# The first FFN's weights are split with ScalarE and adding GpSimd transfers instead of VectorE

## The chip, the core and the metric

The kernel runs on one core of a Trainium2 chip. The metric is device time in microseconds (us) for one execution. Engines are named as in the profile: PE is TensorE, PEld its weight loads, DVE is VectorE, ACT is ScalarE, POOL is GpSimd, SP is SyncE (which here only issues transfers).

## The reference

Two transformer stacks follow each other on 512 tokens of 1024 channels. The part that the change touches is the first of three convolutional FFNs:

```
D_MODEL = 1024; SEQ = 512; D_FF = 2816; CONV_WIDTH = 3
def conv_ffn(x_n, w_up, conv_w, w_down):
    g, u = jnp.split(causal_dwconv(x_n @ w_up, conv_w), 2, axis=-1)
    return (jax.nn.silu(g) * u) @ w_down
...
h = h + short_conv_mixer(rms_norm(h, a_mix_norm[layer]), ...)
h = h + conv_ffn(rms_norm(h, ffn_norm[layer]), ffn_w_up[layer], ffn_conv[layer], ffn_w_down[layer])
```

Behind it come a latent attention, the second FFN, a second block with three mixers, the third FFN and a last norm. All of it is fp32.

## The kernel before

Every matrix product is made of three products with rounded operands. A weight w is split into hi (w rounded to fp32r) and lo = w - hi, an activation x likewise, and PE adds hi·xh, lo·xh and hi·xl into one PSUM bank (`mm3`, L149 to L151; xh and xl are `xsh` and `xsl`, or `hidh` and `hidl`). Tokens lie along the 512 columns of a matmul, channels on the 128 partitions.

Weights come through `slab` (L127 to L145). One SP transfer brings a slab of up to 2048 columns into `raw` (two buffers). Each piece of it is cast by ACT into `whi` (L139) and subtracted by DVE into `wlo` (L141). The pool `wsp` holds two buffers of each, so a piece can be split only when PE is through with the piece two before it.

`ffn(0)` takes its work in two halves of the hidden channels. In the first half it takes 12 slabs of `w_up0` (24 pieces of 1024 columns, each the 8 chunks of one 128-row tile of the product, 24 matmuls) and 8 slabs of `w_down0` (one piece of 1408 columns each, 33 matmuls). In the second half it takes 10 slabs of `w_up0` (20 pieces) and 8 of `w_down0`. That is 60 pieces in all. In this text they are called piece 1 to piece 60 in the order of the code. The last slab of `w_down0` goes to a pool of its own, `late0`. An `evac` behind each tile of `w_up0` multiplies by the norm's factor (DVE), convolves (ACT and DVE), applies silu and splits the hidden rows. In the first half, and at the start of the second, `work` also brings rows of `w_ada` (`ada`, 512 KB each, on SP's queue) and reduces them on DVE (L461).

The order of each engine's instructions is set by the Tile scheduler, which places instructions by priority and by its own estimate of times. Each engine then takes its own list strictly in order. An instruction that waits holds up all that stands behind it on its engine, and for SP and GpSimd these are the transfers that they issue.

Of the kernel before, what the change touches and what calls it, by code (L numbers as in the profile page):

```python
# [19 lines left out]
# What is put between the heads of the stick-breaking attention: slabs of w_out_ac (negative: into a bank  # L20
# of the logits) and weights of what follows.
# [26 lines left out]
class Builder:  # L48
    def __init__(self, ctx, tc, dr, out):
        self.tc, self.nc, self.dr, self.out = tc, tc.nc, dr, out  # L50
        nc = self.nc
        self.ctx = ctx
        self.const = self.pool("const", 1)
        self.wraw = self.pool("wraw", 2)
        self.wsp = self.pool("wsp", 2)
        self.tmp = self.pool("tmp", 1)
        self.small = self.pool("small", 2)

        nc.scalar.preload_act_table(AF.Silu)
        self.par = self.const.tile([P, NPAR], F32, name="par")  # L60
        self.ident = self.const.tile([P, P], F32, name="ident")
        nc.sync.dma_start(self.par[:, :32], dr["params"][:, :32])
        self.mod = self.const.tile([P, 48], F32, name="mod")
        self.probs, self.zms, self.dns = [None] * 6, [None] * 3, [None] * 3
        self.rbs = [None] * 2
        self.hold, self.bufs = None, {}
        self.ones = self.const.tile([P, 1], F32, name="ones")
        nc.vector.memset(self.ones, 1.0)
        self.mhalf = self.const.tile([P, 16], F32, name="mhalf")
        nc.vector.memset(self.mhalf, -0.5)  # L70
        self.h = [self.const.tile([P, T], F32, name=f"h{c}") for c in range(KC)]
# [31 lines left out]
    # Exact two-part split: hi holds 12 significant bits, lo the rest.  # L103
# [23 lines left out]
    def slab(self, src, piece, pool=None, width=PIECE):  # L127
        nc = self.nc
        n = src.shape[-1]
        raw = self.wraw.tile([P, SLAB], F32, tag="raw", name="raw")  # L130
        nc.sync.dma_start(raw[:, :n], src)
        for o in range(0, n, piece):
            own = pool[o // piece] if type(pool) is tuple else pool or self.wsp
            hi = own.tile([P, width], F32R, tag="whi", name="whi")
            lo = own.tile([P, width], F32R, tag="wlo", name="wlo")
            m = min(piece, n - o)
            s = slice(o, o + m)
            with self.tc.issue_after(self.rounded) if self.hold else nullcontext():
                nc.scalar.copy(hi[:, :m], raw[:, s])  # L139
# [13 lines left out]
    def add3(self, ps, wh, wl, xh, xl, first=False):  # L153
        """Onto what products left in the bank, unless it is the first."""
# [4 lines left out]
    def gemm(self, w, xs, evac, slabs=None, group=1, m=0, tag="ps", pool=None):  # L159
        """w: [slabs, 128, m-tiles of a slab x chunks x 128]; evac(m, psum) takes each m-tile from m on."""  # L160
# [11 lines left out]
    def gemm_first(self, w, xs, evac, n):  # L172
        """n m-tiles side by side, their chunks taken as xs yields them."""
# [9 lines left out]
    # Around a norm the tokens go in two halves: one's factors are worked out under the other's products.  # L183
# [3 lines left out]
    def chunks(self, slabs):  # L187
        """The weights of 128 columns after 128 columns, split."""
        return [(hi[:, o:o + P], lo[:, o:o + P]) for hi, lo, n in slabs for o in range(0, n, P)]

    def gemm_halves(self, w, xs, evac):
        """The first m-tiles, chunk by chunk; w: weights by m-tile and chunk, xs[half] yields that half
        of the chunks."""
# [13 lines left out]
    def gemm_last(self, w, xs, evac, done):  # L207
        """The last m-tiles, half by half; w[m]: the weights of each chunk."""
# [10 lines left out]
    def act(self, *args, **kw):  # L219
        """Exp or Ln from the table set that has both."""  # L220
# [3 lines left out]
    # Per-token factors: tokens on the partitions, [128, 4].  # L224
# [40 lines left out]
    def conv(self, x, w, i, n, bias=None):  # L265
        """Causal 3-tap convolution along the tokens; taps of channel tile i in w, n tiles a tap."""
# [20 lines left out]
    def summed(self, add, scales=(None,)):  # L287
        """add, and the squares of h (times each of scales) summed over the chunks as they come;
        those of the last chunk stay apart."""
# [23 lines left out]
    def half_sums(self, half, i=0):  # L313
        """Sums over the channels of a half: tokens on the partitions, [128, 2]."""
# [18 lines left out]
    def half_factor(self, half):  # L333
        """The factors of a half's norm, along the tokens."""
# [4 lines left out]
    def half_factors(self, half):  # L339
        """Two norms in a row: with m1 and m2 the mean squares before and after the first one's gain,  # L340
        (m2 / (m1 + eps) + eps) (m1 + eps) is m2 + eps m1 + eps^2. The first's factor is kept."""
# [52 lines left out]
    def ffn(self, i, xs, rb, add, work=None, done=None, first=None, late=None):  # L394
        """Without rb the normalised rows come whole, and the convolution has a bias."""
# [28 lines left out]
        for half, ys in enumerate(hids):  # L424
            if half:
# [24 lines left out]
    def modulation(self, steps):  # L450
        """shift, scale and gate from c: channels on the partitions, 128 of them in a step."""
# [22 lines left out]
    # Latent attention.  # L474
    def latent(self, w, small, g, dim, ctx, extra=None, pool=None):
        """Normalised latent, its chunks split. With m the mean square of the input's row and l the one
        of the row before the input's factor, (l / (m + eps) + eps) (m + eps) is l + eps (m + eps):
        small is eps (m + eps)."""
# [27 lines left out]
    def swap(self, x):  # L506
        """The halves of each 64 channels, exchanged."""
# [6 lines left out]
    def rope(self, x, cos, sin, after=None):  # L514
        """after: what the vector engine has to do before it takes up the exchanged halves."""
# [126 lines left out]
    def norm_shift(self, gain, shift):  # L642
        """The modulated norm of h, a half after the other: a generator for each."""
# [18 lines left out]
    def gemm_tok(self, w, xs, n, kp, tok):  # L662
        """Tokens on the partitions: w's slabs hold chunks x n columns, kp chunks are split at a time."""
# [12 lines left out]
    def before(self, start):  # L676
        """What is traced inside goes before what was traced since start, where both are ready."""
        return self.tc.high_priority(offset=self.tc.tile_snap_priority() - start)

    def angles(self, pool):  # L680
        """cos and signed sin of position x frequency, the angle reduced to [-pi, pi]."""
# [25 lines left out]
    def gating_in(self, xs, pool):  # L707
# [5 lines left out]
        # Two chunks at a time; the second half behind the first, within what is kept of the weights.  # L713
# [53 lines left out]
    def values(self, ps, npair, pool, tag):  # L767
        """[V of a head | 0 | V of the next] for each pair: a window of 128 columns has one of them."""
# [20 lines left out]
    # Group 0 in the order of the tokens; groups 1 and 2 by the token's rest of a division by 4,  # L789
    # which splits each into four problems of 128 by 128.  # L790
# [57 lines left out]
    def dilated_values(self, vn, vp, y_pool):  # L848
        nc = self.nc
        pool, probs, zms, dns = self.ph, self.probs, self.zms, self.dns  # L850
        # Log-sum-exps, group 0's brought to the order of the others.
# [7 lines left out]
        def reorder(x, sel, keep):  # L859
            """x [128, (head, j)] -> [128, (head, i)]: sel[i] picks rows for each j, keep the j."""  # L860
# [78 lines left out]
    def stick(self, q, k, rows, v, pair, h, out):  # L939
        """Keys on the partitions. The sums over later keys are products with triangles of -1,  # L940
        accumulated onto the logits where they lie."""
# [3 lines left out]
        for t in (2, 1, 0):  # L945
# [3 lines left out]
            # The first product clears the bank for both regions.  # L949
# [34 lines left out]
    def mixer(self, stat):  # L984
        """stat: what holds the sums behind the first norm, open until the bank can go."""
# [105 lines left out]
    def last_phase(self, y_b, wq, held, first, wf0, ctx):  # L1091
        """held: what the mixer's products need, until the last of them."""
# [29 lines left out]
    def final_norm(self, half):  # L1122
        """The rows go out as they are laid: tokens on the partitions, times their factors."""
# [22 lines left out]
    def ffn_phase(self, i, ctx):  # L1146
        self.stat = self.pool(f"stat{i}", 1, ctx, space=PSUM)
        with ExitStack() as ctx:
# [9 lines left out]
            if i == 0:  # L1158
                self.ffn(i, xs, rb, (self.add_h, self.add_h), work, late=self.pool("late0", 1, ctx))
            else:  # L1160
# [4 lines left out]
                self.modulation_end()  # L1165

# [9 lines left out]
def pack(w, per, rows=None):  # L1176
    """[K, N] -> [slabs, 128, per x K/128 x 128]: 128x128 tiles, the contraction on the partitions."""
# [104 lines left out]
```

## Time and profile before

| | before |
|---|---|
| time, median of 3 runs | 1822.06 us (1821.37 to 1825.72) |
| profiled execution, span | 1822.4 us |
| PE busy | 1796.4 us |
| DVE busy | 1110.4 us |
| ACT busy | 698.3 us |
| GpSimd busy | 19.1 us |
| HBM read | 180.27 MB |

The profiled execution is known by its span alone, from its first to its last instruction. It lies 0.3 us above the median of the runs, and no time around the span is given for it. The first FFN begins on PE at 190.1 us and its last product is over before 560 us.

### The profile page before, as it was taken

What the parts mean: (1) busy time and instruction counts of PE and PEld (TensorE: products, weight loads), DVE (VectorE), ACT (ScalarE), POOL (GpSimd) and SP (SyncE); (2) the same over time, 40 slices, a digit from 0 to 9 for tenths busy, and PEclk for the clock granted to TensorE, in tenths of its full rate; (3) what the DMA queues carried; (4) which work ended last, traced back from release to release, by engine and by line L of the source; (5) the groups of instructions that cost most, each with busy time, mean ns of one, the idle gap of its engine ahead of it and who ended that gap; (6) DMA issues with size and microseconds to landing.
All of it is one profiled execution on the core that took longest, in us unless ns stands there. A gap on an engine that the chain in (4) does not pass through costs nothing.

```text
span 1822.4 us, 20686 instructions
## 1 busy us (share of the span) xinstructions
PE 1796.4 (99%) x8301; PEld 1457.3 (80%) x8301; DVE 1110.4 (61%) x1717; ACT 698.3 (38%) x1054; POOL 19.1 (1%) x27
## 2 busy tenths in 40 slices
PE   8999999999999999999999999999999999999998
PEld 6888888888887777787788888887767988888887
DVE  4655699446754676789944775755444765525554
ACT  4323334224434454444422444423354444313432
POOL 0000000000000000000000000100000000000000
PEclk9999999999999999999999999999989999999999
DMA  6222463322231211247332224312101222222222
GB/s 221 93 92 93 162 243 120 111 92 93 94 117 62 76 58 64 99 139 242 125 99 105 93 80 140 100 60 91 61 30 45 82 76 101 81 95 92 94 97 76
DMA packets 38928, 186.59 MB, mean 102 GB/s; under 512 B 5168, under 2 KB 6192, under 8 KB 26672
## 3 DMA queue, kind: packets, MB, share of 16 engines
q1 hardware_dynamic: 36720, 182.38, 29.2%
q10 hardware_dynamic: 2112, 2.89, 0.6%
q8 instruction: 65, 1.06, 0.3%
q14 instruction: 31, 0.25, 0.0%
HBM read 180.27 MB, written 2.10 MB: 100 GB/s over the span
## 4 chain that ended last, share of the span: by engine, by line
PE 93%; DVE 3%; DMA 3%; ACT 1%; issue 1%; SPq 0%; DVEq 0%; POOLq 0%; ACTq 0%
PE ps L149 28%; PE ps L150 28%; PE ps L151 28%; DMA ada<-w_ada 2%; PE z L156 1%; PE z L973 1%; PE sc L149 1%; DVE ada L461 1%; PE o L981 1%; PE sc L151 1%; PE sc L150 1%; DVE wlo L141 1%; PE sc L837 1%; PE pt L630 1%; PE st L932 0%
## 5 line engine op out<-in xcount | busy, mean ns | idle before, releaser
L149 PE MATMUL ps<-xsh,whi 128*128 128x512 f32 (+1 forms) x1432 | 555.7, 393 | 7.9 <-ACT whi L139 6.3
L150 PE MATMUL ps<-xsh,wlo 128*128 128x512 f32 (+1 forms) x1432 | 561.5, 392 | 0.7 <-DVE wlo L141 0.7
L151 PE MATMUL ps<-xsl,whi 128*128 128x512 f32 (+1 forms) x1432 | 559.0, 392 | 0.0
L139 ACT CAST whi<-raw 128x1024 fp32r<-128x1024 f32 (+5 forms) x282 | 296.7, 1057 | 519.5 <-PE ps L151 424.0
L141 DVE TENSOR_TENSOR wlo<-raw,whi 128x1024 fp32r<-128x1024 f32 (+5 forms) x282 | 346.6, 1232 | 110.8 <-ACT whi L139 109.8
L149 PEld LDWEIGHTS ps<-xsh,whi 128*128 128x128 f32 x1432 | 270.5, 189 | 70.1 <-ACT whi L139 6.3
L150 PEld LDWEIGHTS ps<-xsh,wlo 128*128 128x128 f32 x1432 | 270.7, 189 | 64.7 <-DVE wlo L141 2.7
L151 PEld LDWEIGHTS ps<-xsl,whi 128*128 128x128 f32 x1432 | 269.7, 189 | 61.7
L150 PE MATMUL ps<-hidh,wlo 128*128 128x512 f32 (+1 forms) x658 | 244.4, 372 | 0.0
L151 PE MATMUL ps<-hidl,whi 128*128 128x512 f32 (+1 forms) x658 | 244.3, 372 | 0.0
L149 PE MATMUL ps<-hidh,whi 128*128 128x512 f32 (+1 forms) x658 | 244.2, 372 | 0.0
L149 PEld LDWEIGHTS ps<-hidh,whi 128*128 128x128 f32 x658 | 123.8, 188 | 24.0
L150 PEld LDWEIGHTS ps<-hidh,wlo 128*128 128x128 f32 x658 | 123.7, 188 | 23.8
L151 PEld LDWEIGHTS ps<-hidl,whi 128*128 128x128 f32 x658 | 123.7, 188 | 23.7
L274 DVE SCALAR_TENSOR_TENSOR cv<-e,par,cv 128x511 f32<-128x511 f32 (+1 forms) x192 | 141.3, 745 | 2.0 <-ACT cv L270 0.3
L279 DVE TENSOR_TENSOR h<-ps,h 128x512 f32<-128x512 f32 (+1 forms) x75 | 49.9, 668 | 135.3 <-PE ps L151 134.9
L274 DVE SCALAR_TENSOR_TENSOR cv<-ps,par,cv 128x511 f32<-128x511 f32 (+1 forms) x88 | 65.4, 748 | 86.8 <-ACT cv L272 85.2
L406 DVE TENSOR_TENSOR e<-ps,rb 128x512 f32<-128x512 f32 x88 | 60.0, 687 | 65.0 <-PE ps L151 65.0
L118 ACT CAST hidh<-cv 128x512 fp32r<-128x512 f32 x66 | 40.8, 618 | 125.3 <-DVE cv L414 125.3
L270 ACT ACTIVATE cv<-e,par 128x512 f32<-128x512 f32 x96 | 68.7, 719 | 25.0 <-DVE e L406 23.7
L412 ACT ACTIVATE si<-cv 128x512 f32<-128x512 f32 x66 | 41.7, 631 | 73.5 <-DVE cv L274 73.3
L283 DVE SCALAR_TENSOR_TENSOR h<-ps,mod,h 128x512 f32<-128x512 f32 (+1 forms) x38 | 23.9, 635 | 67.9 <-PE ps L151 67.9
(307 smaller groups left out, 1824.6 us busy)
## 6 DMA issues: line engine op xcount, KB each, us to landing
raw<-w_up SPq DMA_DIRECT2D x65, 1024.0 KB, 4.8
raw<-w_down SPq DMA_DIRECT2D x48, 704.0 KB, 4.1
ada<-w_ada SPq DMA_DIRECT2D x48, 512.0 KB, 4.4
raw<-a_w_in SPq DMA_DIRECT2D x9, 1024.0 KB, 4.8
raw<-a_w_out SPq DMA_DIRECT2D x4, 1024.0 KB, 4.7
raw<-w_o SPq DMA_DIRECT2D x4, 1024.0 KB, 5.2
raw<-a_w_in_first SPq DMA_DIRECT2D x8, 384.0 KB, 4.3
raw<-w_uq SPq DMA_DIRECT2D x4, 768.0 KB, 4.8
```

Of the source, the lines that this page charges most:

```text
L118: nc.scalar.copy(vh, src)
L139: nc.scalar.copy(hi[:, :m], raw[:, s])
L141: nc.vector.tensor_tensor(lo[:, :m], raw[:, s], hi[:, :m].bitcast(F32), ALU.subtract)
L149: mm(ps, wh, xh, start=first, stop=False)
L150: mm(ps, wl, xh, start=False, stop=False)
L151: mm(ps, wh, xl, start=False, stop=last)
L270: nc.scalar.activation(y, x, AF.Identity, scale=self.p(w, 2 * n + i))
L274: nc.vector.scalar_tensor_tensor(y[:, k:], x[:, :T - k], self.p(w, (2 - k) * n + i), y[:, k:], ALU.mult, ALU.add)
L279: self.nc.vector.tensor_tensor(self.h[m][:, s], ps, self.h[m][:, s], ALU.add)
L283: self.nc.vector.scalar_tensor_tensor(self.h[m][:, s], ps, self.mod[:, gate + m:gate + m + 1], self.h[m][:, s], ALU.mult, ALU.add)
L406: nc.vector.tensor_tensor(e, ps, rb, ALU.mult)
L412: nc.scalar.activation(st["s"], y, AF.Silu)
```

## The change

In `ffn(0)` alone, `slab` goes by another path. A flag `by_dma` is "rest" in the first half and "all" in the second.

- In "rest", `raw` and the ACT cast into `whi` stay. The remainder is made by ACT, which writes -hi into `wlo`, and by a transfer on GpSimd's queue, which reads the weights from HBM once more and adds them onto `wlo`.
- In "all", there is no `raw` either: a transfer on GpSimd's queue brings the weights into `whi` and rounds them on the way. The remainder is made as in "rest".
- Every third piece goes to a third pair of buffers, the new pool `wsp2`. The pool `late0` is gone. So a piece can now be split when PE is through with the piece three before it.

Other differences between the two files are comments.

```diff
-        raw = self.wraw.tile([P, SLAB], F32, tag="raw", name="raw")
-        nc.sync.dma_start(raw[:, :n], src)
+        if self.by_dma != "all":
+            raw = self.wraw.tile([P, SLAB], F32, tag="raw", name="raw")
+            nc.sync.dma_start(raw[:, :n], src)
         for o in range(0, n, piece):
             own = pool[o // piece] if type(pool) is tuple else pool or self.wsp
+            if self.by_dma and own is self.wsp:
+                self.turn += 1
+                own = self.wsp2 if self.turn % 3 == 0 else own
             hi = own.tile([P, width], F32R, tag="whi", name="whi")
             lo = own.tile([P, width], F32R, tag="wlo", name="wlo")
             m = min(piece, n - o)
             s = slice(o, o + m)
+            if self.by_dma:
+
+                if self.by_dma == "all":
+                    nc.gpsimd.dma_start(hi[:, :m], src[:, s])
+                else:
+                    nc.scalar.copy(hi[:, :m], raw[:, s])
+                nc.scalar.activation(lo[:, :m], hi[:, :m].bitcast(F32), AF.Copy, scale=-1.0)
+                nc.gpsimd.dma_start(lo[:, :m], src[:, s], accum_op=ALU.add)
...
+                continue
...
         for half, ys in enumerate(hids):
+            if i == 0:
+                self.by_dma = ("rest", "all")[half]
...
             if i == 0:
-                self.ffn(i, xs, rb, (self.add_h, self.add_h), work, late=self.pool("late0", 1, ctx))
+                self.wsp2 = self.pool("wsp2", 1, ctx)
+            if i == 0:
+                self.ffn(i, xs, rb, (self.add_h, self.add_h), work)
...
+            self.by_dma = None
```

What this makes of the engines' lists is shown at three places. In the changed file the matmuls of `mm3` are L166 to L168, the negation is L148, the adding transfer L149 and the rounding transfer L145.

**ScalarE, start of the first FFN.** `whi_1367` is piece 1 in both. Piece 2 is `whi_1404` before and `whi_1405` now; piece 3 is `whi_1452` before and `whi_1454` now. `xsh` and `sq` belong to the last chunks of the norm. Before:

```order
L139 CAST whi_1367<-raw_1365 128x1024
L120 ACTIVATE xsh_1315<-h6_85,par_71 128x512
L231 ACTIVATE sq_1340<-h6_85 128x512
L139 CAST whi_1404<-raw_1365 128x1024
L120 ACTIVATE xsh_1319<-h7_86,par_71 128x512
L231 ACTIVATE sq_1343<-h7_86 128x512
L139 CAST whi_1452<-raw_1450 128x1024
```

Now:

```order
L147 CAST whi_1367<-raw_1365 128x1024
L120 ACTIVATE xsh_1315<-h6_85,par_71 128x512
L248 ACTIVATE sq_1340<-h6_85 128x512
L148 ACTIVATE wlo_1368<-whi_1367 128x1024
L147 CAST whi_1454<-raw_1452 128x1024
L148 ACTIVATE wlo_1455<-whi_1454 128x1024
L147 CAST whi_1405<-raw_1365 128x1024
L120 ACTIVATE xsh_1319<-h7_86,par_71 128x512
L248 ACTIVATE sq_1343<-h7_86 128x512
L148 ACTIVATE wlo_1406<-whi_1405 128x1024
```

The negation of piece 1 stands behind two steps of the norm, and piece 3, whose buffers are new, is split ahead of piece 2.

**PE, a border between two pieces in the second half.** Before (`ps_2893` ends and `ps_2938` begins):

```order
L149 MATMUL ps_2893<-xsh_1319,whi_2889 128x512
L150 MATMUL ps_2893<-xsh_1319,wlo_2890 128x512
L151 MATMUL ps_2893<-xsl_1320,whi_2889 128x512
L149 MATMUL ps_2938<-xsh_1291,whi_2934 128x512
L150 MATMUL ps_2938<-xsh_1291,wlo_2935 128x512
L151 MATMUL ps_2938<-xsl_1292,whi_2934 128x512
```

Now, at the same place (`ps_2925` ends; pieces 39 and 40 are `whi_2964` and `whi_3002`):

```order
L166 MATMUL ps_2925<-xsh_1319,whi_2920 128x512
L167 MATMUL ps_2925<-xsh_1319,wlo_2921 128x512
L168 MATMUL ps_2925<-xsl_1320,whi_2920 128x512
L166 MATMUL ps_2969<-xsh_1291,whi_2964 128x512
L166 MATMUL ps_3007<-xsh_1291,whi_3002 128x512
L167 MATMUL ps_2969<-xsh_1291,wlo_2965 128x512
L168 MATMUL ps_2969<-xsl_1292,whi_2964 128x512
```

The first matmul of the second piece of a pair has moved ahead of the first use of the first piece's remainder.

**GpSimd, the same stretch.** Before, it held only norm factors and a few memsets in the whole program, and none of its instructions lay inside the second half:

```order
L244 ISA
L244 TENSOR_TENSOR r<-ms,mhalf 128x4 x6
L244 TENSOR_TENSOR r<-ms_8629,mhalf 128x2
L351 TENSOR_TENSOR r_6097<-m_8628,mhalf 128x2
L771 MEMSET vp 128x2x64 x4
```

Now (pieces 37 to 40, `whi` and `wlo` of a piece bearing neighbouring numbers):

```order
L145 DMA whi_2882<-w_up0 128x1024
L145 DMA whi_2920<-w_up0 128x1024
L149 DMA wlo_2883<-w_up0 128x1024
L149 DMA wlo_2921<-w_up0 128x1024
L145 DMA whi_2964<-w_up0 128x1024
L145 DMA whi_3002<-w_up0 128x1024
L149 DMA wlo_2965<-w_up0 128x1024
L149 DMA wlo_3003<-w_up0 128x1024
```

The adding transfer of the first piece of a pair (`wlo_2965`) stands behind the rounding transfer of the second (`whi_3002`). Pieces 37 to 52 go in eight such pairs, pieces 33 to 36 one by one.

## Rows read from the trace of the kernel before

**Rows 1.** The page's first part: busy us, share of the span, instructions

```profile
PE 1796.4 (99%) x8301; PEld 1457.3 (80%) x8301; DVE 1110.4 (61%) x1717; ACT 698.3 (38%) x1054; POOL 19.1 (1%) x27
```

**Rows 2.** Windows: stretch, length, busy of PE, PEld, DVE, ACT, POOL; clock, DMA share, GB/s

```profile
190.00:312.00 122.00, 122.00 (x533) 98.61 (x532) 105.47 (x154) 48.19 (x63) 1.01 (x1) 1.00 0.55 187
...
324.00:386.00 62.00, 62.00 (x268) 49.94 (x267) 22.74 (x23) 12.46 (x11) 0.00 (x0) 1.00 0.31 104
386.00:498.00 112.00, 112.00 (x482) 90.24 (x481) 75.59 (x95) 44.41 (x57) 0.00 (x0) 1.00 0.25 88
```

**Rows 3.** PE's waits in the whole program: total us, times, longest

```profile
PE ps L149 <- ACT whi L139: 7.2, 2, 6.3
PE st L932 <- DVE yl L123: 3.6, 1, 3.6
PE ps L149 <- ACT lath L118: 2.0, 1, 2.0
PE ps L149 <- DVE h L279: 1.8, 3, 0.9
```

**Rows 4.** Groups by shape, 184 to 560 us, DVE and ACT

```profile
L141 DVE TENSOR_TENSOR wlo<-raw,whi 128x1024 fp32r<-128x1024 f32 x46 | 56.1, 1220 | 16.0 <-ACT whi L139 16.0
...
L141 DVE TENSOR_TENSOR wlo<-raw,whi 128x1408 fp32r<-128x1408 f32 x16 | 25.9, 1625 | 8.9 <-ACT whi L139 8.7
...
L139 ACT CAST whi<-raw 128x1024 fp32r<-128x1024 f32 x46 | 48.3, 1051 | 105.6 <-PE ps L151 93.0 <-issue 12.6
...
L139 ACT CAST whi<-raw 128x1408 fp32r<-128x1408 f32 x16 | 21.9, 1374 | 59.3 <-PE ps L151 48.7 <-issue 5.2 <-DMA raw<-w_down 4.7
```

**Rows 5.** Timeline of GpSimd, and one issue on SP: start, length

```profile
200.72 1.01 POOL L244 TENSOR_TENSOR r<-ms,mhalf 128x4 f32<-128x4 f32 x1 [172.57 <-DVE ms L252]
...
608.32 1.39 POOL L244 TENSOR_TENSOR r<-ms,mhalf 128x4 f32<-128x4 f32 x1 [11.08 <-DVE ms L498]
...
218.60 0.33 SPq L131 DMA_DIRECT2D raw<-w_up  x1
```

**Rows 6.** Transfers issued 190 to 560 us: count, KB each, median us to landing

```profile
raw<-w_up SPq DMA_DIRECT2D x20, 1024.0 KB, 4.8
ada<-w_ada SPq DMA_DIRECT2D x22, 512.0 KB, 4.4
raw<-w_down SPq DMA_DIRECT2D x16, 704.0 KB, 4.1
...
raw<-w_dkv SPq DMA_DIRECT2D x1, 512.0 KB, 3.2
```

**Rows 7.** Timeline of ACT at the start of the first FFN

```profile
184.73 1.05 ACT L139 CAST whi<-raw 128x1024 fp32r<-128x1024 f32 x1 [3.39 <-issue]
185.68 0.72 ACT L120 ACTIVATE xsh<-h,par 128x512 fp32r<-128x512 f32 x1
186.31 0.62 ACT L231 ACTIVATE sq<-h 128x512 f32<-128x512 f32 x1
190.34 1.05 ACT L139 CAST whi<-raw 128x1024 fp32r<-128x1024 f32 x1 [3.42 <-PE ps L151]
```

**Rows 8.** Timeline of PE at the same border

```profile
189.85 0.39 PE L151 MATMUL ps<-hidl,whi 128*128 128x512 f32 x1
190.09 0.39 PE L149 MATMUL ps<-xsh,whi 128*128 128x512 f32 x1
```

**Rows 9.** Windows around two gaps of PE, columns as in rows 2

```profile
600.00:620.00 20.00, 17.97 (x89) 14.64 (x88) 15.13 (x25) 9.45 (x16) 1.39 (x1) 0.98 0.29 88
620.00:632.00 12.00, 11.57 (x55) 9.05 (x54) 7.76 (x14) 4.56 (x10) 0.00 (x0) 0.89 0.03 7
1320.00:1330.00 10.00, 6.37 (x46) 5.74 (x45) 5.47 (x7) 4.57 (x6) 0.00 (x0) 0.96 0.38 121
1330.00:1340.00 10.00, 10.00 (x42) 7.81 (x41) 3.64 (x7) 4.43 (x10) 0.00 (x0) 0.67 0.04 12
1340.00:1350.00 10.00, 10.00 (x40) 7.86 (x41) 5.93 (x12) 5.82 (x12) 0.00 (x0) 0.69 0.00 1
```

More of the change, by code (lines that the diff above doesn't have):

```diff
@@ L65, in __init__ @@
         self.rbs = [None] * 2
-        self.hold, self.bufs = None, {}
+        self.hold, self.bufs, self.by_dma, self.turn = None, {}, None, 0
         self.ones = self.const.tile([P, 1], F32, name="ones")
@@ L137, in slab @@
             s = slice(o, o + m)
+            if self.by_dma:
[5 more added lines that the diff above has]
+                nc.gpsimd.dma_start(lo[:, :m], src[:, s], accum_op=ALU.add)
+                if pool is None:
+                    yield hi, lo
+                else:
+                    yield hi, lo, m
+                continue
             with self.tc.issue_after(self.rounded) if self.hold else nullcontext():
```

## The prediction

> **What bounds the kernel now.** I read the page's busy times first. PE is busy 1796.4 of the 1822.4 us [rows 1], so nothing but 26 us of PE's gaps can be won by relieving another engine. A busy PE need not be at its peak, so I then cut the first FFN into windows and counted matmuls. From 190 to 312 us, where DVE is loaded most (105.5 of 122 us), from 324 to 386, where it is loaded least (22.7 of 62), and from 386 to 498, PE is busy all the time, and 112 us hold 482 matmuls: 0.232 us each, at full clock [rows 2]. The rate does not care what DVE does. Last come PE's waits in the whole program: the long ones are on the first weights of the program (7.2 us), in the second block's attention (3.6) and behind the first FFN, in the latent attention (2.0) [rows 3]. None lies in the stretch whose weights the change splits in another way. There PE uses up a piece of 24 matmuls in 5.57 us and one of 33 in 7.66, and the split keeps ahead of it.
>
> **What is removed.** DVE loses 44 subtractions of 1.220 us (the row counts 46, two belong to the next stage) and 16 of 1.625: 79.7 us [rows 4]. PE waits for none of them, so this is worth nothing by itself.
>
> **What is added off the path.** ACT gains 60 negations, costed like the casts of the same size, 44 × 1.051 + 16 × 1.374 = 68.2 us, and loses the 28 casts of the second half, 20 × 1.051 + 8 × 1.374 = 32.0 [rows 4]. In 112 us of steady state ACT is busy 44.4 [rows 2]; 20 pieces there would bring 21 more. The cover is ACT's idle time, and it holds. SP loses 18 slab loads. GpSimd, nearly empty, gets 88 transfers, and HBM is read once more for each remainder, 34 MB.
>
> **What is added on the path.** The remainder used to be ready 2.3 us after its buffer came free (a cast and a subtraction). Now it goes through a queue and a transfer. No row shows either kind of GpSimd transfer, so three prices are bounded by neighbours:
> - g, GpSimd's own time for one transfer: 0.33 us, as SP's issue, to 1.39, as its slower small power; I take 1.0, its power in this very stage, since it is the same engine [rows 5].
> - H, a 512 KB rounding transfer from there to landing: 3.2 to 4.4 us, the two plain rows of that size; I take 3.2, since the 4.4 was measured amid the `ada` traffic, which is over by then [rows 6].
> - A, a 512 KB adding transfer: 3.2 if adding is free, 9.6 at twice the 1024 KB row; I take 4.8, that row itself, because the transfer has to read 512 KB of weights and 512 KB of what it adds onto [rows 6].
>
> What the Trainium skill says of such an addition, in "Collectives: The Full Stack" (The bandwidth ceiling), is that it is not slow for the arithmetic but because it has two source reads. That fits the choice of A; no row here shows it.
>
> A handover between engines costs 0.1: a matmul that starts at 189.85 and takes 0.39 frees the buffer of a cast that starts at 190.34 [rows 7, 8].
>
> *Start of the FFN.* Piece 1's buffer comes free as before, and its cast starts at 184.73. Two norm steps follow it on ACT and end by 186.9 [rows 7]; the negation ends at 188.0, and the remainder lands at 188.0 + 0.1 + 1.0 + 4.8 + 0.1 = 194.0. PE arrives at 190.09 [rows 8], does one matmul, and then has to do one with piece 2, whose cast cannot start before 190.34 [rows 7]: ready 191.5 instead of 190.3, 1.2 lost. After two more matmuls it is 192.0, and piece 1's remainder is 2.0 late. Sum 3.2 us.
>
> *Pieces 5 to 7.* Piece 3 was taken before piece 2, so piece 5 has one piece less of lead. From the end of piece 2: cast of 5 (to 1.15), of 6 (2.2), one `evac` step of 0.72, negation (3.95), transfer: 9.95. PE meanwhile has 3 matmuls of piece 3, the 24 of piece 4, and one each of 5, 6 and 7; the one of 7 waits for a cast that needs the end of piece 4 (7.5 instead of 6.7, 0.8 lost), and then at 7.75 the remainder of 5 is 2.2 late. Sum 3.0 us.
>
> *Rest of the first half.* Three buffers give 11.1 us from a free buffer to its use. Needed are 0.1 + 1.05 + 0.72 + 1.05 + 0.1 + 1.0 + 4.8 + 0.1 = 8.9. The 2.2 to spare cover it; for 1408 columns there is more to spare. Nothing.
>
> *Second half, pairs.* GpSimd's list is in pairs: rounding a, rounding b, adding a, adding b. Rounding b waits until PE has ended the first piece of the previous pair, and adding a stands behind it. From that moment PE has 23 matmuls of the previous pair's second piece and two first matmuls: 25 × 0.232 = 5.8 us. Adding a lands after 0.1 + 2 × 1.0 + 4.8 + 0.1 = 7.0. So 1.2 us are lost in each of eight pairs: 9.6. Adding b lands in time: 0.1 + 1.0 + 3.2 + 0.1, about 0.35 of another ACT step, a negation 1.05, 0.1 + 1.0 + 4.8 + 0.1 = 11.8, wanted at 5.8 + 1.2 + 5.3 = 12.3. The same chain for pieces 33 to 36, which go one by one, takes 11.8 where 11.4 is there: three times 0.4, with what piles up at the fourth 1.5. The first pair of `w_down0` has 704 KB transfers; A grows there by the slope between the 704 and 1024 KB rows (0.7 per 320 KB, so 0.8 for the 384 KB more that it reads) to 5.6, and is 2.0 late. The later pieces have 7.4 us instead of 5.3 and lose nothing. Sum 13.1 us.
>
> Total 3.2 + 3.0 + 13.1 = 19.3 us on the profiled 1822.4: **1841.7 us**, 1.1% slower. (The median of the runs is 0.3 lower, which I leave out.)
>
> **The rivals.**
>
> *The transfers are hidden (no change).* With g 0.33 and A 3.2 the pairs need 4.1 of 5.8 us, the start 1.2, piece 5 0.8: 2.0 in all, 1824.4. It decides at 2g + A below 5.6. For it speaks that plain 512 KB loads do land in 3.2 [rows 6]; against it, that an addition has to read both operands and that GpSimd takes a microsecond for the smallest operation [rows 5]. The Trainium skill, "DMA: Bandwidth & Descriptors" (Anatomy of one DMA), would put a 512 KB GpSimd transfer at 2.0 us plus its bytes at 436 GB/s, an estimate of 3.2 us. With A at the 3.2 of the row and g at 1.0 only 3.5 us would be lost, 1825.9. Chance of this rival 0.18.
>
> *The transfers are dearer.* With g 1.39, H 4.4 and A 9.6, the start costs 8.4, piece 5 8.2, each of the 17 `w_up0` pieces from 8 to 24 one third of the 3.0 us by which its chain is too long (17), the pairs 6.8 each (54), pieces 33 to 36 about 14, the pair of `w_down0` 8: 110 us, 1932. Two things push that way. From 190 to 312 us the queues already take 0.55 of the DMA engines at 187 GB/s [rows 2], and the remainders add some 94 GB/s of reading, more where `ada` is densest; with the second reads that can fill them, and 2.2 us are all there is to spare. And a gap of PE can cost clock: after 2.5 us of gaps the granted clock was 0.89 for 12 us, and after 3.6 us it was 0.67 and 0.69 for 20 [rows 9], 1.3 and 6.4 us of work; ten gaps at 1.3 would make 13 us, 1855. Chance of 1860 or more 0.30.
>
> *Faster.* Freed of 79.7 us, DVE might bring the end of the FFN forward. Of PE's waits 1.8 us are on DVE's additions to `h`, over three places [rows 3], and in the second block the scheduler's order has changed slightly. To pass the bound of 0.3%, 5.5 us, the 3.6 us gap of the attention and the half clock behind it (6.4) would have to go as well, by an order that happens to be luckier: about 1811. Nothing in the change reaches there directly. Chance 0.06.
>
> **How the numbers follow.** 0.46 for some 1828 to 1860 around 1841.7; 0.18 hidden; 0.30 at 1860 and beyond, about a tenth of it all above 1892; 0.06 faster. About 0.3% is what a measurement of this kernel can tell from no change. Faster 0.06, same 0.18, slower 0.76. The range 1822 to 1892 leaves out about 0.1 on each side.
>
> **What would show it.** Right: in the second half of the FFN (some 370 us wide before, near 390 now) PE waits for transfers of `wlo` about once a pair, for a microsecond or two; at its start it waits for a cast and then a transfer. The landing time of the adding transfers and GpSimd's spacing of neighbouring issues give A and g. Wrong: PE without gaps there means that 2g + A is below 5.6; gaps in the steady first half mean that it is over 8 or that the `ada` traffic delays the transfers. A fall of the clock behind the gaps would be a cost that the sum has not.

## The result, and the profile after

The changed kernel takes **1900.24 us** (median of 4 runs, 1898.52 to 1912.52) against 1821.71 for the kernel before on the same chip: ratio 1.0443, 95% interval 1.0414 to 1.0471. It is 4.4% slower, 78.5 us. The prediction had the sign and most of the places, but 19.3 us, and the result lies beyond its upper bound of 1892.

The profiled execution has a span of 1896.7 us, 74.3 more than before. The busy line of the page after, and windows of the same three kinds as in [rows 2] (dense vector work, `w_down0`, second half; columns as there):

```profile
PE 1821.3 (96%) x8301; PEld 1469.5 (77%) x8301; DVE 1041.8 (55%) x1657; ACT 733.5 (39%) x1086; POOL 88.1 (5%) x115
```

```profile
190.00:312.00 122.00, 104.89 (x433) 82.76 (x434) 74.60 (x118) 56.57 (x70) 16.26 (x19) 0.94 0.94 253
345.00:405.00 60.00, 60.00 (x260) 48.53 (x259) 9.92 (x14) 20.95 (x18) 8.02 (x10) 1.00 0.84 202
425.00:545.00 120.00, 98.98 (x378) 76.26 (x376) 47.31 (x66) 38.74 (x50) 24.47 (x34) 0.91 0.65 141
```

DVE is relieved, 1110.4 to 1041.8 us [rows 1] (68.6 less, where the prediction added up 79.7), and PE does the same 8301 matmuls. But in the first and third window PE is no longer busy all the time, its granted clock is below 1, and in the first the DMA engines are busy 0.94 of the time instead of 0.55 [rows 2]. Only in the stretch of `w_down0` in the first half does PE run as before.

PE's waits in the whole program after (total us, times, longest), which answer to [rows 3]:

```profile
PE ps L167 <- DMA wlo<-w_up: 38.9, 17, 5.3
PE ps L167 <- DMA wlo<-w_down: 8.9, 4, 3.0
PE ps L166 <- ACT whi L156: 7.0, 2, 6.1
PE st L951 <- DVE yl L123: 3.6, 1, 3.6
...
PE ps L166 <- ACT whi L147: 1.6, 2, 0.9
```

The first two rows and the last are new: 49.4 us, with 0.3 more on a rounding transfer 49.7, all in the first FFN (a "gap" is from here on a wait of PE for a weight). 17.2 of it lies in the first half, 32.5 in the second. From the last addition to `h` ahead of the first FFN (at 189.70 us, before 190.28) to the first matmul behind it (632.32, before 562.30, where the last product of the FFN ends at 561.4 and not before 560) are 442.6 us instead of 372.0, 70.6 more. The gaps leave 20.9 of them. Windows of the changed kernel around one of the gaps (5.3 us, until 223.8):

```profile
215.00:219.50 4.50, 2.83 (x11) 1.72 (x10) 4.40 (x9) 3.82 (x7) 1.23 (x2) 1.00 0.98 339
219.50:229.70 10.20, 5.88 (x14) 4.68 (x15) 6.29 (x11) 1.85 (x3) 0.86 (x1) 0.50 1.03 246
229.70:240.00 10.30, 10.30 (x47) 8.41 (x46) 7.14 (x12) 4.87 (x6) 0.86 (x1) 1.00 0.87 284
```

PE waits, and the granted clock is 0.50, 1.2 GHz instead of 2.4, until well after it works again: in the middle row 14 matmuls in 5.88 us, 0.42 each, where the next row has 0.22. I cut the whole FFN into short windows and added up length × (1 - granted clock): 20.4 us, none in the kernel before. Gaps of 49.7 and 20.4 of lost clock make 70.1 of the 70.6. Behind the FFN the changed kernel takes another 4.3 us more (1264.4 against 1260.1). The same sum there is 13.6 us against 10.3, if the last stretch, in which PE has almost nothing to do, is left out; what brings the difference was not tried.

Groups by shape of the FFN after (busy us, mean ns), the prices that [rows 4] and [rows 5] stood in for:

```profile
L148 ACT ACTIVATE wlo<-whi 128x1024 fp32r<-128x1024 f32 x44 | 46.3, 1053 | 62.5 <-DMA whi<-w_up 62.3
L149 POOL DMA_DIRECT2D wlo<-w_up x44 | 38.7, 878 | 343.4 <-ACT wlo L148 342.0 <-PE ps L167 1.0 <-DMA wlo<-w_up 0.4
...
L145 POOL DMA_DIRECT2D whi<-w_up x20 | 14.0, 699 | 60.6 <-PE ps L168 51.6 <-issue 8.9
```

Transfers after, by stretch of issue (count, KB, median us from issue to landing, GpSimd's own time in it), 190 to 262 us and 425 to 545, beside [rows 6]:

```profile
ada<-w_ada SPq DMA_DIRECT2D x15, 512.0 KB, 6.2
raw<-w_up SPq DMA_DIRECT2D x6, 1024.0 KB, 6.7
wlo<-w_up POOLq DMA_DIRECT2D x11, 512.0 KB, 8.8
...
wlo<-w_up POOLq DMA_DIRECT2D x17, 512.0 KB, 5.6
whi<-w_up POOLq DMA_DIRECT2D x16, 512.0 KB, 5.7
```

In the second half, beside rounding transfers but away from the `ada` loads, an adding transfer lands after 5.6 us, amid the `ada` loads after 8.8. These loads and the raw ones have become slower themselves, 6.2 and 6.7 us, where the kernel before has in the same stretch, 190 to 262 us:

```profile
ada<-w_ada SPq DMA_DIRECT2D x17, 512.0 KB, 4.1
raw<-w_up SPq DMA_DIRECT2D x6, 1024.0 KB, 5.6
```

The timeline of the start, engine by engine, where [rows 7] and [rows 8] stood:

```profile
186.24 1.05 ACT L148 ACTIVATE wlo<-whi 128x1024 fp32r<-128x1024 f32 x1
...
187.61 1.05 POOL L149 DMA_DIRECT2D wlo<-w_up  x1 [160.06 <-ACT wlo L148]
...
190.80 0.74 PE L166 MATMUL ps<-xsh,whi 128*128 128x512 f32 x2 [0.90 <-ACT whi L147]
193.24 0.50 PE L167 MATMUL ps<-xsh,wlo 128*128 128x512 f32 x1 [1.71 <-DMA wlo<-w_up]
```

This is the forecast sequence nearly to the tenth: 0.90 on the cast of piece 2 (forecast 1.2), 1.71 on the remainder of piece 1 (2.0).

And one pair of the second half:

```profile
451.30 0.89 POOL L145 DMA_DIRECT2D whi<-w_up  x1
458.59 1.06 ACT L148 ACTIVATE wlo<-whi 128x1024 fp32r<-128x1024 f32 x1 [3.58 <-DMA whi<-w_up]
461.50 0.55 POOL L145 DMA_DIRECT2D whi<-w_up  x1 [9.31 <-PE ps L168]
462.04 0.92 POOL L149 DMA_DIRECT2D wlo<-w_up  x1
468.20 0.87 POOL L149 DMA_DIRECT2D wlo<-w_up  x1 [5.25 <-ACT wlo L148]
468.76 0.87 POOL L145 DMA_DIRECT2D whi<-w_up  x1
...
469.28 0.50 PE L167 MATMUL ps<-xsh,wlo 128*128 128x512 f32 x1 [1.90 <-DMA wlo<-w_up]
```

The negation of piece a is done at 459.65, but its adding transfer starts only at 462.04: ahead of it in GpSimd's list stands the rounding transfer of piece b, which waits until PE has left b's buffer (9.31 us of idle, ended by PE). From 461.50 to PE's first use are 7.8 us, where the prediction had 7.0. At 468.76 the next pair's rounding transfer goes out right behind adding b.

### The profile page after: what moved, and what is told of

It reads as the page before. It is cut to its first block, busy times and chain, and to the rows that moved or that the text cites. A ratio compares the mean times of both kernels' runs of the same rounds, so it can differ in the third digit from the quotient of the medians.

```text
span 1896.7 us, 20827 instructions
## 1 busy us (share of the span) xinstructions
PE 1821.3 (96%) x8301; PEld 1469.5 (77%) x8301; DVE 1041.8 (55%) x1657; ACT 733.5 (39%) x1086; POOL 88.1 (5%) x115
## 4 chain that ended last, share of the span: by engine, by line
PE 78%; issue 10%; DMA 6%; DVE 3%; POOL 2%; ACT 1%; POOLq 0%; DVEq 0%; SPq 0%; ACTq 0%
PE ps L166 23%; PE ps L167 23%; PE ps L168 23%; DMA wlo<-w_up 3%; POOL wlo L149 1%; PE z L173 1%; PE z L992 1%; POOL whi L145 1%; PE sc L166 1%; DMA ada<-w_ada 1%; DVE ada L480 1%; PE o L1000 1%; DVE wlo L158 1%; PE sc L168 1%; PE sc L167 1%
## 5 line engine op out<-in xcount | busy, mean ns | idle before, releaser
L167 PE MATMUL ps<-xsh,wlo 128*128 128x512 f32 (+1 forms) x1432 | 568.7, 397 | 39.2 <-DMA wlo<-w_up 38.9
L166 PE MATMUL ps<-xsh,whi 128*128 128x512 f32 (+1 forms) x1432 | 559.4, 396 | 10.4 <-ACT whi L156 6.1
L168 PE MATMUL ps<-xsl,whi 128*128 128x512 f32 (+1 forms) x1432 | 563.7, 395 | 0.0
L156 ACT CAST whi<-raw 128x1024 fp32r<-128x1024 f32 (+4 forms) x222 | 228.6, 1035 | 360.5 <-PE ps L168 283.8
L166 PEld LDWEIGHTS ps<-xsh,whi 128*128 128x128 f32 x1432 | 273.7, 192 | 75.4 <-ACT whi L156 6.0
L168 PEld LDWEIGHTS ps<-xsl,whi 128*128 128x128 f32 x1432 | 273.2, 191 | 61.5
L158 DVE TENSOR_TENSOR wlo<-raw,whi 128x1024 fp32r<-128x1024 f32 (+4 forms) x222 | 267.3, 1207 | 96.2 <-ACT whi L156 95.6
L168 PE MATMUL ps<-hidl,whi 128*128 128x512 f32 (+1 forms) x658 | 244.7, 373 | 0.0
L166 PE MATMUL ps<-hidh,whi 128*128 128x512 f32 (+1 forms) x658 | 244.1, 373 | 0.0
L166 PEld LDWEIGHTS ps<-hidh,whi 128*128 128x128 f32 x658 | 124.2, 189 | 24.1 <-issue 0.3
L168 PEld LDWEIGHTS ps<-hidl,whi 128*128 128x128 f32 x658 | 124.1, 189 | 23.4
L148 ACT ACTIVATE wlo<-whi 128x1024 fp32r<-128x1024 f32 (+1 forms) x60 | 68.3, 1140 | 100.1 <-DMA whi<-w_up 62.3
L261 POOL TENSOR_TENSOR r<-ms,mhalf 128x4 f32<-128x4 f32 (+2 forms) x13 | 16.8, 1291 | 1284.2 <-DVE ms L1153 375.6
```

Source lines behind the costliest of these rows:

```text
L148: nc.scalar.activation(lo[:, :m], hi[:, :m].bitcast(F32), AF.Copy, scale=-1.0)
L158: nc.vector.tensor_tensor(lo[:, :m], raw[:, s], hi[:, :m].bitcast(F32), ALU.subtract)
L166: mm(ps, wh, xh, start=first, stop=False)
L167: mm(ps, wl, xh, start=False, stop=False)
L168: mm(ps, wh, xl, start=False, stop=last)
```

## The experiments

The table has all runs: the median of each and its ratio to the kernel before on the same chip, the gaps of PE in the first FFN on weights (as in the waits above), and the lost clock there, summed over short windows as above. Their sum, which is of the profiled execution, is compared with the loss of the median.

| run | median us | ratio (95%) | gaps | lost clock | sum | loss |
|---|---|---|---|---|---|---|
| the change | 1900.24 | 1.0443 (1.0414 to 1.0471) | 49.7 | 20.4 | 70.1 | 78.5 |
| e1_second_half | 1869.48 | 1.0258 (1.0243 to 1.0274) | 29.7 | 18.7 | 48.4 | 47.7 |
| e2_first_half | 1847.29 | 1.0133 (1.0115 to 1.0151) | 18.7 | 6.9 | 25.6 | 25.5 |
| e3_adds_only | 1847.33 | 1.0143 (1.0109 to 1.0176) | 14.9 | 8.5 | 23.4 | 25.6 |
| e4_buffer_only | 1820.48 | 0.9994 (0.9985 to 1.0003) | 0 | 0 | 0 | -1.3 |
| e5_no_ada | 1833.08 | 1.0062 (1.0047 to 1.0077) | 6.7 | 1.7 | 8.4 | 10.6 |
| e6_plain | 1831.45 | 1.0058 (1.0036 to 1.0081) | 6.4 | 3.4 | 9.8 | 9.0 |
| e7_staggered | 1877.68 | 1.0307 (1.0284 to 1.0330) | 34.3 | 20.4 | 54.7 | 55.2 |
| e8_four | 1864.03 | 1.0229 (1.0206 to 1.0251) | 31.5 | 11.9 | 43.4 | 41.6 |
| e9_gaps | 1839.61 | 1.0090 (1.0075 to 1.0105) | 12.1 | 5.2 | 17.3 | 16.7 |
| e10_ahead | 1827.63 | 1.0019 (1.0008 to 1.0030) | 0 | 0 | 0 | 4.8 |
| e11_all_ahead | 1831.09 | 1.0051 (1.0036 to 1.0067) | 3.7 | 1.7 | 5.4 | 8.2 |

### Which half, which part

The edit of the first three is one line, the mode of each half; in e1, e2 and e4, and in e5 to e7 below, the third buffer is also taken whatever the mode. e4 has `(None, None)`.

```
-                self.by_dma = ("rest", "all")[half]
+                self.by_dma = (None, "all")[half]      # e1_second_half
+                self.by_dma = ("rest", None)[half]     # e2_first_half
+                self.by_dma = ("rest", "rest")[half]   # e3_adds_only
```

> First half as before the change (ScalarE's cast, VectorE's subtraction), second half changed, three buffers in both. Theory A (late transfers, each half by itself, and half clock behind the gaps): in the trace of the change the second half takes 221.3 us from addition to addition against 173.4 before, so this kernel loses about 48 us, and up to 4 more in the attention: 1868 to 1876 us. Theory B (the new order and the new buffers cost, not the transfers): 1895 to 1900, as the whole change. Theory C (the second half suffers only because the first has left it late and at half clock): below 1850.

> First half changed (cast on ScalarE, negation, adding transfer), second half as before the change, three buffers in both. Theory A: the first half takes 226.1 us against 203.4, so 22.7 lost and up to 4 in the attention: 1843 to 1849 us, with the gaps between 190 and 300 us, where the ada loads run, and none after. Theory B: 1895 to 1900. Theory D (a steady chain that is too long whatever else runs): gaps in the first half's w_down pieces too, 1855 or more.

> Adding transfers in both halves, no rounding transfers: ScalarE casts in the second half as well. Theory A (the rounding transfer, 5.6 us to landing, and GpSimd's paired list are what the second half loses by; an adding transfer without ada traffic lands in 5.5 us): the chain of a piece is 0.1 + 1.05 + 0.72 + 1.05 + 0.1 + 5.5 + 0.1 = 8.6 of 11.1 us, the second half has no gaps, and the loss is the first half's: 1843 to 1849 us. Rival E (the adding transfers are what is late in both halves): the second half still loses 20 us or more, 1865 to 1895.

> The split as before the change in both halves, but with the third pair of buffers in place of the one kept for the last piece. Theory A: no wait for a transfer is left, 1820 to 1825 us. Theory B (order and buffers): 1835 or more. If the longer lead wins anything at all it shows here as less than 1816.

All four came out where theory A had them. The two halves lose almost independently: 47.7 + 25.5 = 73.2 of 78.5, and the gaps 29.7 + 18.7 = 48.4 of 49.7. The third buffer costs nothing, nor does taking piece 3 ahead of piece 2, which e4 does too; the order of the pairs on PE was not tried alone. And with adding transfers alone the second half loses nothing: windows of e3_adds_only from 330 to 545 us,

```profile
330.00:430.00 100.00, 100.00 (x434) 81.17 (x433) 25.97 (x37) 45.35 (x45) 13.20 (x16) 1.00 0.81 192
430.00:545.00 115.00, 115.00 (x499) 93.34 (x498) 53.66 (x75) 67.11 (x79) 16.43 (x19) 1.00 0.81 192
```

PE is busy throughout at full clock, with 28 adding transfers in the second half. So rival E falls: what the second half loses by comes with the rounding transfers.

### The first half: traffic or chain?

In e5 the load of `ada` is made once; in e6 GpSimd's transfer overwrites the remainder instead of adding onto it. In both only the first half is changed.

```
+            if i >= 24 or i == steps[0]:               # e5_no_ada
                 nc.sync.dma_start(w, self.dr["w_ada"][i])
...
-                nc.gpsimd.dma_start(lo[:, :m], src[:, s], accum_op=ALU.add)
+                nc.gpsimd.dma_start(lo[:, :m], src[:, s])   # e6_plain
```

> Only the first half changed, as in the run e2_first_half (1847.3 us, gaps 17.1 us on wlo and 1.6 on casts), and of the 24 ada loads only the first is made; VectorE multiplies that one slab 24 times, so the modulation sums are left out and the time of VectorE stays. Theory A (the ada traffic delays the adding transfers): they land in some 5.5 us instead of 7.8, the steady gaps between 240 and 300 us go, piece 5's 5.3 shrinks to 2 or 3, the start's 3.3 stays: 1827 to 1835 us. Rival F (the chain through GpSimd is too long whatever else is moved): 1843 to 1849, landing as before.

> Only the first half changed, and the transfer behind the negation overwrites the remainder instead of adding onto it (so the remainder is not computed), with all ada loads as before. Theory G (the addition's second read is what makes the transfer long): landing in some 5 us instead of 7.8, gaps at the start only, 1826 to 1833 us. Rival F (GpSimd's queue and the reading of HBM cost, not the addition): landing above 7 us and 1843 to 1849. In between, the part that the addition has is read off.

Theories A and G were right at once, and rival F falls. The transfer row of the 512 KB remainders issued between 190 and 330 us, in e2_first_half, e5_no_ada and e6_plain:

```profile
wlo<-w_up POOLq DMA_DIRECT2D x21, 512.0 KB, 8.4
```

```profile
wlo<-w_up POOLq DMA_DIRECT2D x23, 512.0 KB, 6.2
```

```profile
wlo<-w_up POOLq DMA_DIRECT2D x22, 512.0 KB, 4.8
```

Without the `ada` loads 2.2 us less, without the addition 3.6 less, and in each case the steady gaps are gone or nearly so (on transfers, e5 keeps 1.8 at the start, 3.0 for piece 5 and 0.3 behind; e6 keeps 3.6 for piece 5, then 0.3 and 0.9). The queue rows of the page tell why: packets, MB and share of 16 engines' time of GpSimd's queue, in e2_first_half (span 1846.6), e5_no_ada (1831.2) and e6_plain (1827.4),

```profile
q0 software_dynamic: 4608, 18.35, 5.5%
```

```profile
q0 software_dynamic: 4608, 18.35, 5.6%
```

```profile
q0 software_dynamic: 4608, 18.35, 3.1%
```

The same packets and bytes, and with the addition 1.8 times the engines' time (5.5% × 1846.6 against 3.1% × 1827.4). It is as much without the `ada` loads (5.6% × 1831.2), so it belongs to the addition and not to the traffic around it. That gives an estimate, in time summed over the 16 engines, of what is asked of them per piece: in its 5.57 us they have 89 us. Before the change 0.55 of it is taken [rows 2], 49 us. An adding transfer of 512 KB takes 46 more (its share of the 18.35 MB), 95 in all, which is too much; an overwriting one 26, 75 in all. An `ada` load, about one to a piece, takes 22 (SP's queue has 28.4% of 1846.6 us in e2 and, with 23 loads fewer, 26.9% of 1831.2 in e5), so without it and with the addition some 73 are left. The two cures are two ways back below 89: from 190 to 312 us the engines are busy 0.78 of the time in e5 and 0.79 in e6, where the change has 0.94.

The Trainium skill, "Collectives: The Full Stack" (The bandwidth ceiling), says that an addition on the way has two source reads where a copy has one, and gives a measured ratio of 1.93 for a collective that adds against one that copies. The 1.8 here agrees with it. For a plain GpSimd transfer the Trainium skill, "DMA: Bandwidth & Descriptors" (Anatomy of one DMA), would give an estimate of 3.2 us at 512 KB. e6 has 4.8 amid the `ada` loads, and the measurement decides.

### The second half: GpSimd's list

In e7 an order is imposed on the list, one rounding transfer ahead, with three buffers. e8 is the whole change with a fourth buffer for `w_up0`, and the scheduler's own order.

```
+            with self.tc.issue_after(last) if last else nullcontext():   # e7_staggered
+                r = nc.gpsimd.dma_start(hi[:, :m], src).ins
+            if old:
+                last = self.rest(old, r)     # negation; adding transfer after r
+                yield old[:2]
...
+                if piece == D:                                           # e8_four
+                    own, width = ((own, PIECE), (own, PIECE), (self.wsp2, PIECE), (self.wsp3, D))[self.turn % 4]
```

> Only the second half changed, as in e1_second_half (1869.5 us, 14 gaps on wlo of 29.0 us), but GpSimd's list is staggered: the rounding transfer of the next piece goes ahead of each adding transfer, and no second one. Theory A (pairs: an adding transfer stands behind a rounding one whose buffer is not free, and the next rounding one behind the pair's last adding one): the chain of one piece is 0.1 + 0.55 + 5.0 + 0.1 + 1.05 + 0.1 + 0.9 + 5.0 + 0.1, 12.9 us of 11.1, 0.6 lost a piece in the steady state, 12 in all, and with some half clock 1833 to 1846 us. Rival H (the transfers are too slow in any order, or too many): 1860 to 1875.

> The whole change with a fourth pair of buffers for the 1024-column pieces, so that 16.7 us instead of 11.1 lie between a free buffer and its use; the 1408-column pieces keep three. Theory A (what is lost is the time of single transfers, not what the DMA engines can move): no gap in the w_up pieces of either half but at the start (about 3) and little for piece 5; w_down of the second half still loses some 10: 1833 to 1848 us. Rival I (the first half is limited by what the DMA engines can move, busy 0.99 between 232 and 262 us): the gaps between 240 and 300 us stay, 1848 to 1860. Rival F: 1880 or more.

Both of my numbers were wrong: e7 lies above both ranges, nearer to rival H, and e8 lies above those of theory A and rival I. In e7 I had costed the chain of one piece and forgotten the list again: there *every* adding transfer stands behind a rounding transfer that waits for a buffer, not every second one. GpSimd's timeline in e7_staggered:

```profile
416.93 0.56 POOL L172 DMA_DIRECT2D whi<-w_up  x1 [7.49 <-PE ps L194]
417.47 0.91 POOL L188 DMA_DIRECT2D wlo<-w_up  x1
422.53 0.56 POOL L172 DMA_DIRECT2D whi<-w_up  x1 [4.15 <-PE ps L194]
423.07 0.91 POOL L188 DMA_DIRECT2D wlo<-w_up  x1
```

Each adding transfer leaves in the same moment as the rounding one ahead of it, and that one was released by PE. From the release at 416.93 to PE's first use at 425.17, the end of a gap of 2.7 us, are 8.2 us, and PE had 5.57 us of work left. In e8 the waits are turned round. GpSimd's timeline there:

```profile
456.11 0.88 POOL L152 DMA_DIRECT2D wlo<-w_up  x1 [6.40 <-ACT wlo L151]
459.97 0.87 POOL L152 DMA_DIRECT2D wlo<-w_up  x1 [2.97 <-ACT wlo L151]
460.51 1.44 POOL L148 DMA_DIRECT2D whi<-w_up  x2
468.06 0.88 POOL L152 DMA_DIRECT2D wlo<-w_up  x1 [6.11 <-ACT wlo L151]
```

Rounding transfers no longer wait for buffers (0.8 us once from 425 to 525), but two of them stand behind both adding transfers of the pair before, which wait for the negations: 12 us a cycle where PE uses a pair up in 11.1, so still 0.6 to 1.6 lost a pair. And of the first half, which e8 starts without a gap (PE busy all the time from 190 to 262 us), theory A was only half right: behind it, in e8_four,

```profile
262.00:300.00 38.00, 30.55 (x124) 23.82 (x123) 26.64 (x44) 18.23 (x24) 5.18 (x6) 0.91 0.99 280
```

the DMA engines are full (0.99), and PE has gaps of 6.6, 0.5, 0.3 and then 3.1 us. A longer lead puts the gaps off and does not remove them. Rival I holds for this stretch. Another gap of 5.8 us lies in `w_down0` of the first half (until 356.7), where e8 has three buffers again; it was not followed up. With it the first half has 16.3 us of gaps, little less than the 17.2 of the change.

e10 gives the second half both: the staggered list, drawn through `w_up0` and `w_down0` in one, and four buffers, the fourth in the idle raw slabs. e11 has the whole change with that, a fourth buffer in the first half, and the `ada` load of e5.

```
+        pools = [(self.wsp, PIECE), (self.wsp, PIECE), (self.wsp2, PIECE), self.fourth]
+        i = min((i for i in range(4) if m <= pools[i][1]), key=lambda i: self.used[i])
...
+                    src = self.ahead([up[s][:, o:o + D] for s in r for o in (0, D)] + [down[s] for s in range(KC, 2 * KC)])
```

> Only the second half changed, as in e1_second_half (1869.5 us) and e7_staggered (1877.7), with the staggered list of the latter (rounding of the next piece, then adding of this one) and a fourth pair of buffers, which are the two raw buffers that lie idle there. Theory M (an adding transfer stands in GpSimd's list behind a rounding transfer that waits for a buffer): with four the rounding transfer of the next piece waits for the end of a piece that lies 11.1 us before the use, and 0.1 + 0.55 + 0.9 + 5.9 = 7.5 is needed: no gaps, 1820 to 1827 us. Rival H (the transfers are too slow or too many in any order): gaps stay, 1840 or more.

> The whole change with everything named as a cause taken away: four pairs of buffers in both halves (for 1024 columns in the first), the staggered list in the second, and of the ada loads of this FFN only the first (VectorE multiplies the one slab 24 times; the modulation sums are left out). All 88 transfers of GpSimd are still made. Theories A and M together: no gap on a transfer but at the start (at most 3 us), 1820 to 1828 us. Rival (something else in the change costs as well): 1835 or more.

The window of the second half in e10_ahead, and GpSimd's timeline in it:

```profile
390.00:545.00 155.00, 155.00 (x670) 125.74 (x669) 66.98 (x95) 60.11 (x77) 35.01 (x49) 1.00 0.90 201
```

```profile
447.92 0.56 POOL L181 DMA_DIRECT2D whi<-w_up  x1 [3.98 <-PE ps L199]
449.34 0.86 POOL L193 DMA_DIRECT2D wlo<-w_up  x1 [0.86 <-ACT wlo L191]
453.52 0.56 POOL L181 DMA_DIRECT2D whi<-w_up  x1 [3.32 <-PE ps L199]
454.38 0.86 POOL L193 DMA_DIRECT2D wlo<-w_up  x1 [0.30 <-issue]
```

PE never waits, at full clock, although the DMA engines are busier (0.90) than in the change (0.65) and the adding transfers land later (7.6 us, median of those issued from 390 to 520, against 5.6). Theory M holds and rival H falls: the second half lost by the order of the list and the lead, not by the transfers. The median, 0.6 us above the range of theory M, still loses 4.8 us. In the FFN the profile has neither a gap nor lost clock, so they are looked for behind it: there PE waits 3.2 us for remainders of VectorE's split (0.7 before), 2.2 of them once, at 835.7 us, far behind the change. What brings that wait and the rest was not tried. In e11_all_ahead one gap on a transfer is left in the FFN, at the start,

```profile
PE ps L198 <- DMA wlo<-w_up: 3.7, 1, 3.7
```

and 1831.1 us, three above what I expected, with all 88 transfers made. The gap and its clock are 5.4 of the 8.2 us lost; the other 2.8 are open, and nothing larger is hidden in the change.

### The clock, without transfers

e9 starts from the kernel before. Of its pieces of `w_up0` in the second half, every second one goes into the buffer that the piece ahead of it has just left.

```
+            if self.pairs and piece == D:
+                own, width = ((self.ga, D), (self.gb, PIECE))[self.turn // 2 % 2]
+                self.turn += 1
```

> The split of the kernel before, without any transfer of GpSimd, but every second 1024-column piece of the second half is put into the buffer that the piece right before it has just left. PE then waits for a cast and, one matmul later, for a subtraction: 0.1 + 1.05 + 0.1 + 1.22 + 0.1 less that matmul, 2.3 us in each of 10 pairs, 23 us. Theory K (gaps of PE cost clock whatever causes them): half-clock stretches behind the gaps as in e1_second_half, where 29 us of gaps went with a loss of 47.7: here 33 to 42 lost, 1855 to 1864 us. Rival L (the half clock in the changed kernel has another cause, such as the transfers): 1843 to 1847, at full clock.

The gaps were smaller than I worked out, 12.1 us over nine (PE's waits of e9_gaps, 380 to 545 us), all on casts; the wait for the subtraction that I had added does not show:

```profile
PE ps L152 <- ACT whi L142: 12.1, 9, 1.9
```

so my number was too high, but the lost clock is there, and without any GpSimd transfer. Windows of the same run behind two gaps of 1.85 and 1.86 us:

```profile
442.00:449.00 7.00, 5.70 (x18) 4.52 (x19) 6.32 (x9) 3.65 (x6) 0.00 (x0) 0.76 0.47 152
479.00:486.00 7.00, 5.14 (x16) 3.84 (x15) 6.80 (x9) 3.86 (x6) 0.00 (x0) 0.76 0.30 106
```

The time lies below both ranges, so the clock decides here and not the time: gaps of 12.1 and 5.2 of lost clock make 17.3 for a loss of 16.7. Rival L falls, since the half clock came behind gaps on casts, in a kernel without GpSimd transfers. Theory K holds with a limit: the clock fell behind three of the eight places with gaps, at 443, 481 and 529 us, and not behind the others. e4 and e10, which have no gap in the FFN, lose no clock there.

No run beat both kernels, and none of these experiments points to a way: PE has no gap in this FFN before the change.

## Why the prediction was wrong

**What bounds the kernel.** Right: relieving DVE of 69 us bought nothing, and in the FFN 70.1 of the 70.6 us lost are gaps of PE or its clock.

**The start.** Right: 2.6 us measured for 3.2.

**g and A.** Right away from the `ada` loads: GpSimd's own time is 0.88 us (1.0 assumed), and g + A of 5.8 stands against 5.6 in the second half.

**"Rest of the first half … Nothing."** This is the step that failed first, in the order of the code. The chain of 8.9 us in 11.1 was right, but for an adding transfer away from the `ada` loads. Amid the `ada` loads it lands after 8.8 instead of 5.8, the chain is 11.9, and the 2.2 us to spare are gone: five gaps, 8.6 us, which go without these loads (e5) and all but go without the addition (e6). The prediction named this in its dearer rival, with the right two reasons, the share of 0.55 and the second reads, and left it out of the sum. What it could have worked out from [rows 2]: 0.55 of the engines moved 187 GB/s, so a copy of 512 KB takes some 25 us of their time and an addition at twice the reads 49. With the 49 already taken that is 98 of the 89 us that 16 engines have in a piece of 5.57 us. (The 46 measured for the addition make it 95.) Piece 5 belongs here: 6.0 us for pieces 5 to 7 instead of 3.0 (0.73 on a cast, 5.25 on the remainder), since 2.2 us late plus 3.0 of slower transfer is 5.2.

**The pairs of the second half.** Mechanism right: a rounding transfer that waits for its buffer, and an adding one behind it. Size off: a gap of 1.9 in the pair shown instead of 1.2, since the adding transfer took 7.2 us beside the rounding one instead of 5.8; and in other pairs up to 3.7. The sum did not follow that the next rounding transfer stands behind adding b in turn (468.76 above); how much of the rest comes of it was not worked out. `w_up0` lost 23.7 us there instead of 11.1.

**H.** Mis-sized: g + H was 4.2 and measured 5.7. The plain row of 512 KB was the wrong neighbour. The lead that it cost may be part of what `w_down0` of the second half lost, 8.9 us instead of 2.0; that was not tried alone.

**Clock loss 0 in the sum.** The largest single error: 20.4 us, as much as the whole forecast. The sum gave no reason for the nothing. The dearer rival had 1.3 a gap, 13 for ten gaps; there were 24 gaps, and 20.4.

Gaps of 49.7 for 19.3, and 20.4 for 0: the first a matter of traffic and order, the second a consequence that [rows 9] had shown. Of the 59.2 us that the forecast lacks, 20.4 are clock, 12.6 the pairs, 8.6 the steady first half, 6.9 `w_down0`, 3.0 pieces 5 to 7, and the start has 0.6 too much. The other 8 or so lie mostly behind the FFN (4.3) and between the profiled execution and the median (4.2).

## What to carry to other kernels

An engine's queue is a list in order: when a transfer that waits for a buffer stands ahead of one that is ready, cost the pair from the buffer's release, and give it buffers enough that the one it waits for is free early (e7 against e10: four instead of three, and one list through both weights, 50 us). Before moving work onto DMA, add up the engines' time in the busiest stretch, an addition counted at almost two copies (1.8 here); a lead covers a late transfer (e10), but not engines that are full (e8). And when PE is the bound, price a new gap at its length plus the half clock behind it: 41% more in the changed kernel, 25 to 63% in the runs that lost clock.

## What was not expected of the hardware

An adding transfer took 1.8 times the DMA engines' time of an overwriting one of the same bytes, and landed after 5.6 us away from the `ada` loads and after up to 11.5 amid them.

The half clock does not follow from the length of a gap alone. In the changed kernel nine of the fourteen gaps of 1.87 to 5.25 us went with some 3 to 10 us at half clock; five did not, one of 2.97 us (until 562.3) among them. The two gaps at the start, 0.90 and 1.7 us, cost no clock in the changed kernel and 1.7 us of it in e2_first_half. In e8, where eight gaps of 0.6 to 1.6 us lay between 414 and 524 us, the clock from 425 to 525 was 1.00. What decides was not tried.
